# One reciprocal of two columns for the softmax sums of two neighbouring query tiles

## The chip, the cores and the metric

The kernel runs on one core of one Trainium2 chip. The metric is the time of one execution on the device in microseconds (us); lower is better. Engines are named as in the profile: PE (TensorE matmuls), PEld (its weight loads), DVE (VectorE), ACT (ScalarE), POOL (GpSimd) and SP (SyncE, which issues all DMAs here). A tile is 128 partitions wide; PSUM is used as eight tiles of 128x512 fp32 that the matmuls write into.

## The reference

One encoder layer is applied to two sequences of 512 tokens, with 1024 channels. The input is normalised, one wide product `h @ w_in` feeds four mixers (pooling, attention, convolution, Fourier) with their gates, the four branches are projected up, gated and summed, and an output product with a second normalisation follows. The change lies in the attention:

```
def attend(qblk):
    s = jnp.einsum('bqhd,bkhd->bhqk', qblk, k, preferred_element_type=jnp.float32) * scale
    p = jax.nn.softmax(s, axis=-1).astype(v.dtype)
    return jnp.einsum('bhqk,bkhd->bqhd', p, v)
```

There are 8 heads and, for each head of each sequence, 4 query tiles of 128 rows against 512 keys: 2 x 8 x 4 = 64 softmax tiles of 128x512.

## The kernel before, in words

Every fp32 product is made of three fp32r products of high and low halves (`mm3`), so nearly every operand is split first: `split(hi, lo, src)` copies the high half on ACT and subtracts it on DVE; where the source lies in SBUF and not in PSUM, the subtraction may go to DVE or POOL (`either`).

Work is written down as a program of units, in an order that weaves the long products (the bulk) with the side work. The layer runs in stages: input products of both sequences (to about 563 us of the profile), then the merge products of the four branches with the attention of sequence 0 and then of sequence 1 woven between them, then seven output products (`out_product`, in the order 1, 2, 7, 6, 5, 4, 3) and for each tile the last normalisation and residual (`final`).

For one softmax tile (head `h`, query tile `qt`) three units matter, with other work between them:

- `s_unit` multiplies queries and keys into a PSUM tile, takes the row maximum on DVE (TENSOR_REDUCE into `nmx`) and the exponential on ACT into `pr`, which also writes the row sum into `sm` (ACTIVATE and its ACTIVATION_READ_ACCUMULATOR).
- `n_unit` takes the reciprocal of the sum on DVE and multiplies `pr` by it. The multiplication may run on DVE (TENSOR_SCALAR) or ACT (ACTIVATE with scale): `rec.choice` leaves that to the planner.
- `t_unit` transposes `pr` on PE into PSUM and splits the result into `ph` and `pl` for the product with the values, `pv_unit`.

In `attention` the units of one step stand as s(h, qt), t(h-1, qt), n(h, qt): a tile is normalised just after its scores, and its transposes come four steps later.

The order on each engine isn't the program's. `_Recorder` records each operation as an atom with its dependences; `hoist` moves loads ahead, and `plan` then lists the atoms anew: it gives each a due time, keeps a clock for each engine with estimated durations, and takes next what is ready and most due. It picks the engine of every `choice`, and the buffers (caps: 42 halves of large tiles `b`, 16 tiles `g`, 10 small tiles `s`, 8 PSUM tiles). So one removed instruction can change what stands in a row on an engine, or which engine does it, hundreds of microseconds later. All recorded operations are issued by one line, L182, so the profile's groups are told apart by tiles: `ps` is PSUM, `b` large tiles, `g` tiles of 128x512, `s` small columns.

Of the kernel before, what the change touches and what calls it, by code (L numbers as in the profile page):

```python
# [14 lines left out]
AF = mybir.ActivationFunctionType  # L15
ALU = mybir.AluOpType
# [463 lines left out]
def trunk_kernel(ctx: ExitStack, tc: tile.TileContext, a: dict):  # L480
# [4 lines left out]
    rec = _Recorder()  # L485
# [9 lines left out]
    act, dve, pool, pe, sync = (Engine(e) for e in ("act", "dve", "pool", "pe", "dma"))  # L495
# [14 lines left out]
    def g_(dt=F32, w=512):  # L510
        return rec.new("g", (P, w), dt)
# [7 lines left out]
    def s_(w=1):  # L519
        return rec.new("s", (P, w), F32)  # L520

    def psum(tag):
        return rec.new("ps", (P, 512), F32)
# [45 lines left out]
    def mm3(out, lh, ll, rh, rl, first, last, **kw):  # L569
        pe.matmul(out, lh, rh, start=first, stop=False, **kw)  # L570
        pe.matmul(out, lh, rl, start=False, stop=False, **kw)
        pe.matmul(out, ll, rh, start=False, stop=last, **kw)
# [27 lines left out]
    def build(s):  # L600
        st = {}
# [16 lines left out]
        def Unit(fn, cost=0.0, chunks=()):  # L618
            return _Unit(fn, cost, [(0 if c[0] in SHARED or c[0] == "u" and c[1] < 6 else s,) + c for c in chunks])
# [3 lines left out]
        def after(*keys):  # L623
            assert all(k in done for k in keys), keys
# [248 lines left out]
        def s_unit(h, qt):  # L873
            def fn():
                after("kr0", "kr1", ("k", h // 2))
                qh, ql = [st["q", h // 2][:, h % 2, i] for i in range(2)]
                k = st["k"]
                t = slice(qt * P, (qt + 1) * P)
                p = psum("sc")
                mm3(p, qh[:, t], ql[:, t], k[:, h % 2, 0, :], k[:, h % 2, 1, :], True, True)  # L880
                nmx, sm, rc = s_(), s_(), s_()
                dve.tensor_reduce(nmx, p, axis=AX.X, op=ALU.max, negate=True)
                pr = g_()
                act.activation(pr, p, AF.Exp, bias=nmx, accum_out=sm)
                st["p", h, qt] = (pr, sm)
            return Unit(fn, 0.65)

        def n_unit(h, qt):
            def fn():
                pr, sm = st["p", h, qt]  # L890
                rc = s_()
                dve.reciprocal(rc, sm)
                rec.choice(dve=("tensor_scalar", (pr, pr, rc, None), dict(op0=ALU.mult)),
                           act=("activation", (pr, pr, AF.Copy), dict(scale=rc)))
            return Unit(fn, 0.0)

        def t_unit(h, qt):
# [939 lines left out]
```

## Time and profile before

| | us |
|---|---|
| median of 3 runs | 923.95 (922.61 to 928.17) |
| the profiled execution | 927.52 |
| its span, first to last instruction | 925.7 |
| PE busy | 898.8 (97%) |
| DVE busy | 721.9 (78%) |
| ACT busy | 492.2 (53%) |
| POOL busy | 359.4 (39%) |

The profiled execution is 1.8 us longer than its span, and 3.6 us longer than the median of the runs. Busy time counts overlapping instructions of an engine once; the duration of a single short DVE instruction overlaps with the next one, so the distance between two starts tells what it takes in a row of instructions.

### The profile page before, as it was taken

Reading aid. Unit: us, or ns where it says so; the run is one execution under the profiler, and the core shown is the slowest. Engines: PE = TensorE matmul, PEld = TensorE weight load, DVE = VectorE, ACT = ScalarE, POOL = GpSimd, SP = SyncE. Lnnn points to the kernel's source line nnn. Section 1 sums busy time; section 2 is a strip of 40 time slices with the busy share of each in tenths; the row PEclk is TensorE's granted clock in tenths of the full one; section 3 lists DMA queues with packets and bytes.
Section 4 is the critical chain, followed back from the end, with each engine's and each line's share of the span. In section 5 each row is a group of like instructions: output and inputs, shape, how many; then the busy total and the mean of one; then the engine's idle time right before and its main releaser. Section 6 shows DMA issues by size and latency. Waiting matters only on the chain. (4 is left out here: it accounts for less than half of the span.)

```text
span 925.7 us, 12147 instructions
## 1 busy us (share of the span) xinstructions
PE 898.8 (97%) x4125; PEld 725.4 (78%) x4125; DVE 721.9 (78%) x1089; ACT 492.2 (53%) x871; POOL 359.4 (39%) x305
## 2 busy tenths in 40 slices
PE   7999999999999999999999999899999999999996
PEld 6897877888778888877888887787778777777784
DVE  6889999689994655667634367978899778899998
ACT  7964233345443345435444456855676678873253
POOL 2798432126331322346100031412353344246935
PEclk9999999999999999999999999999999999999998
DMA  7140123332232333543322447866754564461124
GB/s 273 64 152 10 58 103 125 129 110 103 91 125 106 128 133 130 173 142 118 136 104 102 141 141 179 254 217 198 233 186 133 161 242 148 155 231 58 37 101 182
DMA packets 62258, 129.86 MB, mean 140 GB/s; under 512 B 6890, under 2 KB 10483, under 8 KB 61684
## 3 DMA queue, kind: packets, MB, share of 16 engines
q1 hardware_dynamic: 62196, 129.09, 41.7%
q8 instruction: 32, 0.52, 0.2%
q14 instruction: 30, 0.25, 0.1%
HBM read 88.56 MB, written 37.36 MB: 136 GB/s over the span
## 5 line engine op out<-in xcount | busy, mean ns | idle before, releaser
L182 PE MATMUL ps<-b,b 128*128 128x512 f32 (+3 forms) x3428 | 808.1, 392 | 9.9 <-DVE b L182 4.7
L182 PEld LDWEIGHTS ps<-b,b 128*128 128x128 f32 (+1 forms) x3428 | 626.5, 187 | 158.0 <-DVE b L182 6.7
L182 ACT ACTIVATE b<-b 128x1024 fp32r<-128x1024 f32 (+9 forms) x164 | 141.3, 880 | 127.6 <-PE ps L182 46.4
L182 POOL TENSOR_TENSOR b<-b,b 128x512 fp32r<-128x512 f32 (+4 forms) x79 | 120.8, 1542 | 141.1 <-ACT b L182 134.5
L182 DVE TENSOR_TENSOR b<-b,b 128x512 fp32r<-128x512 f32 (+5 forms) x167 | 144.5, 892 | 31.6 <-ACT b L182 30.6
L182 POOL TENSOR_TENSOR b<-g,b 128x512 fp32r<-128x512 f32 x48 | 69.0, 1442 | 133.3 <-ACT b L182 133.3
L182 DVE TENSOR_TENSOR g<-ps,g 128x512 f32<-128x512 f32 (+4 forms) x101 | 66.2, 658 | 63.6 <-PE ps L182 35.8
L182 ACT ACTIVATE g<-ps 128x512 f32<-128x512 f32 (+5 forms) x110 | 59.4, 542 | 88.3 <-PE ps L182 71.9
L182 DVE TENSOR_TENSOR b<-ps,b 128x512 fp32r<-128x512 f32 (+2 forms) x128 | 85.0, 682 | 21.2 <-ACT b L182 20.4
L182 DVE SCALAR_TENSOR_TENSOR ps<-b,cols,ps 128x512 f32<-128x512 f32 x116 | 87.3, 752 | 2.7
L182 ACT ACTIVATE b<-g 128x512 fp32r<-128x512 f32 x101 | 61.5, 629 | 32.3 <-DVE g L182 18.5
L182 ACT ACTIVATE b<-ps 128x512 fp32r<-128x512 f32 (+2 forms) x116 | 66.5, 593 | 19.9 <-PE ps L182 19.2
L182 DVE TENSOR_TENSOR b<-b 128x512 f32<-128x512 f32 (+4 forms) x69 | 61.9, 898 | 9.0 <-POOL g L182 4.0
L182 ACT ACTIVATE g<-ps,s 128x512 f32<-128x512 f32 (+1 forms) x77 | 48.5, 639 | 23.8 <-DVE s L182 14.9
L182 ACT ACTIVATE g<-g,cols 128x512 f32<-128x512 f32 x48 | 34.6, 721 | 48.7 <-DVE g L182 48.3
L182 POOL TENSOR_TENSOR b<-b 128x512 f32<-128x512 f32 (+3 forms) x32 | 43.7, 1367 | 39.2 <-DVE b L182 16.2
L182 POOL TENSOR_TENSOR b<-b,g 128x512 f32<-128x512 f32 x26 | 37.2, 1436 | 51.1 <-DVE g L182 36.0
L182 DVE TENSOR_TENSOR b<-g,b 128x512 fp32r<-128x512 f32 x53 | 51.2, 980 | 4.6 <-ACT b L182 4.1
L182 PE MATMUL ps<-b 128*128 128x512 f32 (+1 forms) x216 | 52.1, 388 | 1.2 <-DVE b L182 1.2
L182 POOL TENSOR_TENSOR g<-b 128x512 f32<-128x512 f32 x15 | 20.1, 1342 | 80.5 <-DMA b<-in_wt 47.7
L182 DVE TENSOR_REDUCE s<-ps 128x1 f32<-128x512 f32 x64 | 43.4, 681 | 4.9 <-PE ps L182 4.5
L182 PEld LDWEIGHTS ps<-b 128*128 128x128 f32 x216 | 39.5, 188 | 9.7 <-issue 1.4
(74 smaller groups left out, 563.4 us busy)
## 6 DMA issues: line engine op xcount, KB each, us to landing
st<-g SPq DMA_DIRECT2D x104, 256.0 KB, 2.0
b<-in_wt SPq DMA_DIRECT2D x50, 512.0 KB, 4.7
g<-st SPq DMA_DIRECT2D x100, 256.0 KB, 3.4
b<-in_x SPq DMA_DIRECT2D x15, 512.0 KB, 4.5
b<-in_wup SPq DMA_DIRECT2D x14, 512.0 KB, 4.5
b<-st SPq DMA_DIRECT2D x4, 1024.0 KB, 6.8
b<-in_wo SPq DMA_DIRECT2D x8, 512.0 KB, 6.7
out_y<-b SPq DMA_DIRECT2D x16, 256.0 KB, 2.1
```

The costliest lines, as they stand in the source:

```text
L182: getattr(engines[atom.eng], method)(*[real(x) for x in args], **{k: real(x) for k, x in kw.items()})
```

## The change

`s_unit` of an even query tile makes a small tile of two columns; the exponentials of the even and the odd tile write their sums into its two columns. `n_unit` of an even tile now does nothing; that of the odd tile takes one reciprocal of both columns and then multiplies both tiles, each by its own column.

```
-                nmx, sm, rc = s_(), s_(), s_()
+                nmx = s_()
+                if qt % 2 == 0:
+                    st["sm", h, qt // 2] = s_(2)
+                sm = st["sm", h, qt // 2][:, qt % 2:qt % 2 + 1]
...
         def n_unit(h, qt):
             def fn():
-                pr, sm = st["p", h, qt]
-                rc = s_()
-                dve.reciprocal(rc, sm)
-                rec.choice(dve=("tensor_scalar", (pr, pr, rc, None), dict(op0=ALU.mult)),
-                           act=("activation", (pr, pr, AF.Copy), dict(scale=rc)))
+                if qt % 2:
+                    rc = s_(2)
+                    dve.reciprocal(rc, st["sm", h, qt // 2])
+                    for i in range(2):
+                        pr, r = st["p", h, qt - 1 + i][0], rc[:, i:i + 1]
+                        rec.choice(dve=("tensor_scalar", (pr, pr, r, None), dict(op0=ALU.mult)),
+                                   act=("activation", (pr, pr, AF.Copy), dict(scale=r)))
```

The planner's new lists begin to differ at the first softmax tile and keep the same work: 64 reciprocals of one column become 32 of two; of the 64 multiplications 18 stand on DVE and 46 on ACT, where 8 and 56 stood; of the operations that may run on DVE or POOL, 33 went from DVE to POOL and 23 from POOL to DVE. On PE 726 of 740 groups of matmuls keep their place in the order; nine of the others stand one place earlier, and five stand one to four places later.

On DVE, at the first softmax tiles of sequence 0. `s_701` is the maximum of tile 0 of head 0, and the rows that follow are the maxima, reciprocals and multiplications of the next tiles; SCALAR_TENSOR_TENSOR is the low half of a query product. Before:

```order
L182 TENSOR_REDUCE s_701_4573<-ps_699_4565 128x1
L182 TENSOR_REDUCE s_703_4579<-ps_700_4569 128x1
L182 TENSOR_REDUCE s_709_4594<-ps_702_4575 128x1
L182 RECIPROCAL s_713_4604<-s_705_4582 128x1
L182 SCALAR_TENSOR_TENSOR b_706_4584<-ps_691_4507,b_706_4584 128x512
L182 TENSOR_REDUCE s_715_4615<-ps_708_4590 128x1
L182 RECIPROCAL s_718_4621<-s_712_4602 128x1
L182 TENSOR_REDUCE s_719_4623<-ps_710_4597 128x1
L182 RECIPROCAL s_720_4632<-s_717_4619 128x1
L182 TENSOR_SCALAR g_716_4618<-g_716_4618,s_720_4632 128x512
```

After:

```order
L182 TENSOR_REDUCE s_701_4573<-ps_699_4565 128x1
L182 TENSOR_REDUCE s_703_4579<-ps_700_4569 128x1
L182 TENSOR_REDUCE s_709_4594<-ps_702_4575 128x1
L182 SCALAR_TENSOR_TENSOR b_706_4584<-ps_691_4507,b_706_4584 128x512
L182 TENSOR_REDUCE s_714_4613<-ps_708_4590 128x1
L182 RECIPROCAL s_715_4616<-s_705_4582 128x2
L182 TENSOR_REDUCE s_716_4618<-ps_711_4599 128x1
L182 TENSOR_SCALAR g_712_4603<-g_712_4603,s_715_4616 128x512
```

The reciprocal of tile 0 is gone from its place; one of two columns stands where that of tile 1 stood, and the multiplication on DVE is now that of tile 1.

On DVE, in the output products, from the evacuation of product 6 on. The rows that read `ps` evacuate a PSUM tile twice (each into another sum); the others are low halves of operands of products 5, 4 and 3 (`b_1480_7703<-b_1414_7419` in the first list and `b_1448_7934` in the second are that of w_out's chunk 0 for product 4, the operand that product 4 needs first). Before:

```order
L182 TENSOR_TENSOR b_1510_8001<-b_1453_7550,b_1510_8001 128x512
L182 TENSOR_TENSOR b_1510_8001<-b_884_5313,b_1510_8001 128x512
L182 TENSOR_TENSOR b_1511_8010<-b_1446_7531,b_1511_8010 128x512
L182 TENSOR_TENSOR b_1511_8010<-b_884_5313,b_1511_8010 128x512
L182 TENSOR_TENSOR b_1499_7907<-ps_1501_7922,b_1499_7907 128x512
L182 TENSOR_TENSOR b_1407_7395<-ps_1501_7922,b_1407_7395 128x512
L182 TENSOR_TENSOR b_1512_8017<-b_1416_7433,b_1512_8017 128x512
L182 TENSOR_TENSOR b_1480_7703<-b_1414_7419,b_1480_7703 128x512
L182 TENSOR_TENSOR b_1499_7907<-ps_1502_7926,b_1499_7907 128x512
L182 TENSOR_TENSOR b_1407_7395<-ps_1502_7926,b_1407_7395 128x512
```

After:

```order
L182 TENSOR_TENSOR b_1436_7812<-ps_1438_7827,b_1436_7812 128x512
L182 TENSOR_TENSOR b_1351_7311<-ps_1438_7827,b_1351_7311 128x512
L182 TENSOR_TENSOR b_1436_7812<-ps_1439_7831,b_1436_7812 128x512
L182 TENSOR_TENSOR b_1351_7311<-ps_1439_7831,b_1351_7311 128x512
L182 TENSOR_TENSOR b_1428_7720<-b_1390_7454,b_1428_7720 128x512
L182 TENSOR_TENSOR b_1436_7812<-ps_1440_7835,b_1436_7812 128x512
L182 TENSOR_TENSOR b_1351_7311<-ps_1440_7835,b_1351_7311 128x512
L182 TENSOR_TENSOR b_1436_7812<-ps_1441_7839,b_1436_7812 128x512
L182 TENSOR_TENSOR b_1351_7311<-ps_1441_7839,b_1351_7311 128x512
L182 TENSOR_TENSOR b_1442_7894<-b_871_5292,b_1442_7894 128x512
L182 TENSOR_TENSOR b_1447_7929<-b_1357_7344,b_1447_7929 128x512
L182 TENSOR_TENSOR b_1448_7934<-b_1354_7328,b_1448_7934 128x512
```

The low half that product 4 needs first stood behind two evacuations of product 6; it now stands behind all eight.

On POOL, over the same stretch: the low halves for products 5, 4 and 3, from the first that reads chunk 3 of the summed operands on. Before:

```order
L182 TENSOR_TENSOR b_1480_7703<-b_808_4987,b_1480_7703 128x512
L182 TENSOR_TENSOR b_1512_8017<-b_884_5313,b_1512_8017 128x512
L182 TENSOR_TENSOR b_1513_8046<-b_1453_7550,b_1513_8046 128x512
L182 TENSOR_TENSOR b_1513_8046<-b_875_5282,b_1513_8046 128x512
L182 TENSOR_TENSOR b_1518_8114<-b_1518_8114,g_1366_7223 128x512 x2
```

After:

```order
L182 TENSOR_TENSOR b_1417_7608<-b_797_4963,b_1417_7608 128x512
L182 TENSOR_TENSOR b_863_5263<-b_863_5263,b_790_4940 128x512
L182 TENSOR_TENSOR b_1417_7608<-b_797_4963,b_1417_7608 128x512
L182 TENSOR_TENSOR b_1442_7894<-b_1390_7454,b_1442_7894 128x512
L182 TENSOR_TENSOR b_1428_7720<-b_1385_7438,b_1428_7720 128x512
L182 TENSOR_TENSOR b_1408_7558<-b_871_5292,b_1408_7558 128x512
L182 TENSOR_TENSOR b_1447_7929<-b_871_5292,b_1447_7929 128x512
L182 TENSOR_TENSOR b_1448_7934<-b_863_5263,b_1448_7934 128x512
L182 TENSOR_TENSOR b_1449_7952<-b_863_5263,b_1449_7952 128x512
L182 TENSOR_TENSOR b_1451_7986<-b_1357_7344,b_1451_7986 128x512
L182 TENSOR_TENSOR b_1451_7986<-b_863_5263,b_1451_7986 128x512
L182 TENSOR_TENSOR b_1417_7608<-b_863_5263,b_1417_7608 128x512
```

Three operations stood between the low half of product 5's chunk 2 (the first row of each list) and the first multiplication by the output gain (the last row before); twelve stand there now (one more follows the rows shown), ten of them moved from DVE.

## Rows read from the trace of the kernel before

**Rows 1.** The page of the profile: busy time of the engines, and busy tenths of PE and DVE in 40 equal slices of the span (23 us each).

```profile
PE 898.8 (97%) x4125; PEld 725.4 (78%) x4125; DVE 721.9 (78%) x1089; ACT 492.2 (53%) x871; POOL 359.4 (39%) x305
...
PE   7999999999999999999999999899999999999996
...
DVE  6889999689994655667634367978899778899998
```

**Rows 2.** Busy time of each engine in stretches of the span, which begin where the softmax begins: first and last us and the length, then PE, PEld, DVE, ACT and POOL, the granted clock of PE, the share of the DMA engines and GB/s.

```profile
563.00:600.00 37.00, 34.09 (x169) 26.93 (x168) 32.22 (x56) 30.75 (x63) 13.32 (x12) 1.00 0.81 227
600.00:720.00 120.00, 118.29 (x621) 95.03 (x620) 104.53 (x184) 77.34 (x150) 38.31 (x32) 1.00 0.59 191
720.00:760.00 40.00, 37.71 (x175) 28.22 (x173) 30.52 (x57) 28.93 (x57) 18.35 (x14) 1.00 0.67 219
760.00:840.00 80.00, 78.59 (x390) 62.23 (x389) 70.95 (x116) 61.87 (x125) 35.04 (x26) 1.00 0.48 162
840.00:900.00 60.00, 59.91 (x259) 48.14 (x258) 58.29 (x72) 24.91 (x52) 40.06 (x27) 1.00 0.21 71
```

**Rows 3.** What PE waited for from 563 us to the end: total us, times, longest.

```profile
PE ps L182 <- DVE b L182: 5.5, 9, 1.7
PE ps L182 <- ACT g L182: 1.2, 2, 0.6
...
PE ps L182 <- DVE g L182: 0.4, 1, 0.4
PE ps L182 <- DVE s L182: 0.4, 1, 0.4
```

**Rows 4.** The timeline of PE: start, us of the merged piece, instructions; in brackets the idle time before it and what ended it. Waits behind the softmax's start.

```profile
587.54 3.74 PE L182 MATMUL ps<-b,b 128*128 128x512 f32 x14 [0.25 <-DVE b L182]
...
596.87 2.33 PE L182 MATMUL ps<-b,b 128*128 128x512 f32 x9 [1.75 <-DVE b L182]
...
739.81 0.95 PE L182 MATMUL ps<-b,b 128*128 128x512 f32 x3 [0.59 <-ACT g L182]
...
752.38 2.35 PE L182 MATMUL ps<-b,b 128*128 128x512 f32 x9 [0.81 <-DVE b L182]
...
822.04 5.74 PE L182 MATMUL ps<-b 128*128 128x512 f32 x24 [1.16 <-DVE b L182]
```

**Rows 5.** Groups of instructions by shape from 563 us to the end, on DVE (two rows) and ACT (one): busy us and mean ns of one, then the idle time before them and what ended it.

```profile
L182 DVE RECIPROCAL s<-s 128x1 f32<-128x1 f32 x64 | 9.6, 153 | 1.6 <-ACT g L182 1.4
L182 DVE TENSOR_SCALAR g<-g,s 128x512 f32<-128x512 f32 x8 | 5.5, 689 | 0.3
...
L182 ACT ACTIVATE g<-g,s 128x512 f32<-128x512 f32 x56 | 40.4, 722 | 12.5 <-DVE s L182 12.4
```

**Rows 6.** The timeline of DVE at the first softmax tiles of sequence 0, and some 26 us later where the low half of a transposed tile (`b<-ps,b`) stands behind a small copy.

```profile
568.05 0.15 DVE L182 RECIPROCAL s<-s 128x1 f32<-128x1 f32 x1
568.12 0.69 DVE L182 TENSOR_REDUCE s<-ps 128x1 f32<-128x512 f32 x1
568.78 0.16 DVE L182 RECIPROCAL s<-s 128x1 f32<-128x1 f32 x1
568.98 0.49 DVE L182 TENSOR_SCALAR g<-g,s 128x512 f32<-128x512 f32 x1
...
594.34 1.80 DVE L182 COPY g<-g 128x2 f32<-128x2 f32 x1
596.05 0.68 DVE L182 TENSOR_TENSOR b<-ps,b 128x512 fp32r<-128x512 f32 x1
```

**Rows 7.** The first transposes of a softmax tile on PE, of sequence 0 and of sequence 1, and between them the reciprocal on DVE of tile 1 of sequence 1.

```profile
571.48 0.60 PE L182 MATMUL ps<-ident,g 128*128 128x128 f32 x4
...
726.53 0.15 DVE L182 RECIPROCAL s<-s 128x1 f32<-128x1 f32 x1
...
729.66 0.60 PE L182 MATMUL ps<-ident,g 128*128 128x128 f32 x4
```

**Rows 8.** DVE groups by shape in two stretches of the output products: from 868 to 881 us, in which POOL works without a break, and from 881.5 to 886 us, in which it rests.

```profile
L182 DVE TENSOR_TENSOR b<-b,b 128x512 f32<-128x512 f32 x3 | 5.3, 1780 | 0.0
L182 DVE TENSOR_TENSOR b<-ps,b 128x512 f32<-128x512 f32 x4 | 2.5, 676 | 0.0
...
L182 DVE TENSOR_TENSOR b<-b,b 128x512 fp32r<-128x512 f32 x7 | 4.3, 686 | 0.1
```

**Rows 9.** The timelines of POOL and PE there.

```profile
865.86 14.83 POOL L182 TENSOR_TENSOR b<-b,b 128x512 f32<-128x512 f32 x9
886.21 1.30 POOL L182 TENSOR_TENSOR b<-b,b 128x512 fp32r<-128x512 f32 x1 [5.52 <-ACT b L182]
...
883.83 2.91 PE L182 MATMUL ps<-b,b 128*128 128x512 f32 x12
...
894.73 0.85 PE L182 MATMUL ps<-b,b 128*128 128x512 f32 x3
```

**Rows 10.** The end of the timelines of PE and DVE.

```profile
916.07 0.84 PE L182 MATMUL ps<-b 128*128 128x512 f32 x3
...
916.98 0.68 DVE L182 TENSOR_TENSOR b<-b,b 128x512 f32<-128x512 f32 x1
917.59 0.68 DVE L182 TENSOR_TENSOR b<-ps,b 128x512 f32<-128x512 f32 x1
...
919.78 2.73 DVE L182 SCALAR_TENSOR_TENSOR b<-b,s,b 128x512 f32<-128x512 f32 x4
```

## Prediction, written before the changed kernel ran

> **What bounds the kernel now.** The page comes first: PE is busy for 97% of the span, in every slice but the first and last few, and DVE for 78% [rows 1]. The change touches nothing ahead of the first softmax tile at 563 us, where the two lists of instructions are still the same, so only the rest counts. There the table by stretches gives PE's idle time as length less busy time: 37.0 - 34.1 = 2.9 us, then 1.7, 2.3, 1.4 and 0.1 us, together 8.4 us of 337 [rows 2]. PE is the bound from 563 to 900 us, and what is not PE's own work is those 8.4 us and the tail behind its last matmul. What ends PE's waits is nearly always DVE: 5.5 + 0.4 + 0.4 us of them, and 1.2 us are ACT's exponentials [rows 3]. Most of the waiting matmuls need a PSUM tile that DVE has not yet emptied [rows 4]. DVE is also nearly full at the end: 58.3 of 60 us from 840 to 900 us [rows 2].
>
> That bounds the gain before any detail: if every one of those waits went, 8.4 us or 0.9% would be won. A loss has no such bound.
>
> The prediction is made against the profiled execution, 927.5 us with a span of 925.7 us; the median of the runs lies 3.6 us lower, and the same difference is put on it.
>
> **The change part by part.**
>
> *Reciprocals.* 32 of 64 go. Each is listed with 153 ns [rows 5], but behind one the next instruction starts 0.07 us later (568.05 to 568.12 us, rows 6), so DVE is freed of 32 x 0.07 = 2.2 us, not of 4.9. The remaining ones have two columns; no row has one of that shape. From below it costs what one column does, from above it costs twice the 0.07 us, which would take the 2.2 us back. I take the lower end, because DVE rows of 512 columns take 0.68 us, about 1 ns a column. Spread over 260 us of attention, 2.2 us of DVE reach PE only where they stand in the row that leads to one of DVE's eleven waits: a few times 0.07, under 0.5 us.
>
> The Trainium skill ("Perfetto Trace Analysis", section Optimizing Scalar/DVE Operations) says that grouping small operations into larger ones helps if the engine is saturated, and that where it is not but causes bubbles elsewhere, breaking instructions up may finish work sooner. By the first half the gain would be the 2.2 us of DVE; by the second the pair is a loss, which is the third rival.
>
> *The added wait.* The even tile's multiplication now waits for the odd tile's exponential. Behind it, on ACT or DVE, stand exponentials, evacuations and splits in order. Who needs the even tile first is its transpose on PE. In sequence 0 the reciprocal of tile 1 ran at 568.05 us [rows 6] and the transposes of tile 0 began at 571.48 us; in sequence 1 these are 726.53 and 729.66 us [rows 7]. That is 3.4 and 3.1 us of cover. I followed all 32 pairs so: these two are the smallest, every other has 4.9 us or more. One reciprocal and two multiplications of 0.72 us [rows 5] take 1.6 us, so the wait is hidden, at no cost. If the two smallest covers failed, each would cost its part over 3 us.
>
> *Fewer waits on ACT.* ACT stood idle 12.4 us in front of its 56 multiplications, waiting for reciprocals [rows 5]. Now the second of a pair finds its column ready, so up to half, 6 us of ACT, is given back, and exponentials may come earlier. PE's waits for exponentials are 1.2 us in all [rows 3]; I credit none here, 1.2 us at most.
>
> *Multiplications to DVE.* Ten more stand on DVE. One took 0.49 us where it ran undisturbed [rows 6] and 0.69 in the mean [rows 5]: 5 to 7 us more on DVE. The operations that went to POOL, ten more than came back, free DVE of 10 x 0.6 = 6 us. With the 2.2 us of the reciprocals DVE's load in total falls by 1 to 3 us, and order decides, not load.
>
> The Trainium skill ("SBUF — State Buffer", section Who interferes with whom) says that of DVE operations with one SBUF input just copies and tensor_scalar can take the port pair that GpSimd needs, and that the later of the two then waits for the whole of the other. By that the ten multiplications would each meet POOL; the mean of 0.69 against 0.49 us fits for some of the eight, and if all ten waited for a POOL operation of 1.3 us the sum would be 10 us higher on DVE, not on PE.
>
> *560 to 600 us.* PE's wait of 1.75 us at 596.87 ended when DVE had emptied a transposed tile at 596.05 to 596.73, which had stood behind a copy of two columns that took 1.80 us [rows 4, 6]. In the new list this split stands ahead of that copy: up to 1.2 us won. Ahead of the first value product (587.54 us) stand now two low halves of the Fourier table on DVE, which POOL did before: 2 x 0.6 us, up to 1 us lost in its wait of 0.25. Net -0.3 us, from -1.3 to +1.0.
>
> *600 to 720 us.* A multiplication now stands on DVE in front of the split that the value product of head 2 waits for: +0.4 us; nothing else that PE waited for has moved. Taken +0.2, from -0.5 to +1.0.
>
> *720 to 760 us.* In front of the first split of sequence 1 stand two low halves that POOL did; DVE had idle time there (30.5 of 40 us busy, rows 2). The exponential that PE waited 0.59 us for at 739.81 [rows 4] now stands behind one more evacuation on ACT, +0.5 us; against that, the large split ahead of the wait of 0.81 us at 752.38 starts sooner. Net 0, from -1.0 to +1.2.
>
> *760 to 840 us.* The wait of 1.16 us at 822.04 [rows 4] is for a split on DVE which had one multiplication and two reciprocals in front of it that are gone, while one evacuation of 0.6 us has come: -0.5 us, from -1.2 to +0.8.
>
> *840 to 900 us.* Ten low halves go from DVE to POOL. What that costs is in rows 8: a DVE operation with both inputs in SBUF took 1.78 us while POOL worked without a break [rows 8, 9], and 0.69 us while it rested; one that reads PSUM took 0.68 us even then. The two engines take turns in such operations. POOL needs 14.83 / 9 = 1.65 us each in such turns, and 1.30 alone [rows 9]. Now POOL has work from 880 to beyond 897 us, so the DVE operations of that stretch fall into turns. The operand that product 4 needs first, at 894.73 us [rows 9], is now split behind all eight evacuations of product 6. Its last four PSUM tiles are done between 883.83 and 883.83 + 2.91 = 886.7 us, the first at about 884.7. DVE empties each twice, at 0.6 us: eight times make 4.8 us, one low half between them 0.6 to 1.7, so 890.1 to 891.2; then three low halves at 0.6 to 1.7: 891.9 to 896.3. PE wants it at 894.73: from 0 to 1.6 us of a new wait. I take +0.8. POOL's own last operand for product 4 is the seventh from 882.9 us, at 1.3 to 1.74 each 892 to 895 us: no more than that.
>
> *Tail.* PE's last matmul ends at 916.9 us, and its evacuation started only at 917.59 us, behind another operation [rows 10]. It now stands directly behind the small column that it had followed at a distance, and may start 0.5 us sooner; but two residual operations that had been done by then come behind it, 0.60 + 0.66 us, ahead of the last four of 2.73 us. Net +0.4 us, from -0.5 to +1.0.
>
> **Sum:** -0.3 + 0.2 + 0 - 0.5 + 0.8 + 0.4 = +0.6 us; ends -4.5 and +6.6 us if all fell together. The profiled execution would take 928.1 us, the median 924.5 us. What separates this kernel from no change in a measurement is about 1%, 9.2 us, so this is no change.
>
> **The rivals.**
>
> 1. *Slower: POOL and DVE in turns.* 33 operations moved to POOL, and each DVE operation that meets one costs 1.78 - 0.68 = 1.1 us more [rows 8]. It decides only where such an operation leads to a matmul or to the last store. If from 870 us on it delays DVE by 9 such turns on PE's path, the time is 924 + 10 = 934 us. For it: DVE is 97% busy there [rows 2], with little slack. Against it: ten operations left DVE there, and only three of the remaining ones lie on the path to product 4. Chance 0.05.
>
> 2. *Faster: DVE's waits go.* DVE ended 6.3 of the 8.4 us [rows 3]; if the new order and the lighter row remove two thirds, 4 us, of them and nothing comes instead, the time is 920 us, still within 1%. For it: the longest wait has its cause, the 1.80 us copy, moved behind. Against it: what was in front of other splits is only exchanged for other work. Chance 0.15. More than 9.2 us is out of reach of the 8.4 us, unless the tail shortens too: 0.02.
>
> 3. *Pairs come late.* The even tile's result is held back for the odd one's, and its transposes wait. The cover is 3.1 us at the least [rows 6, 7]; if both first heads lost 2 us each and the busy ACT queues of the following heads two more, the time is 924 + 6 = 930 us. Chance 0.08, since a pair needs 1.6 us. It is what the second half of the rule on grouping in the Trainium skill ("Perfetto Trace Analysis") amounts to.
>
> **How the numbers follow.** The forecast itself has 0.70: 924.5 us, from about 921 to 928. With rival 2 below and rival 3 above, the range that leaves out no more than 2 in 10 is 919.5 to 929.5 us: below, nearly the whole -4.5 us of the sum; above, most of the +6.6 us, less the unlikely case that all ends meet. Rival 1 (0.05) lies outside. Faster by over 1%: 0.02. Slower by over 1%: 0.05, rival 1. Within 1%: 0.93, the forecast, rival 3 and nearly all of rival 2.
>
> **What would show it.** In the profile after: RECIPROCAL x32 with a mean near 153 ns; no wait of PE's transposes (`ps<-ident,g`) on ACT or DVE `g`; PE's idle time from 563 to 900 us again near 8.4 us, with the 1.75 us wait at 597 us shorter; a new wait of PE near 895 us ended by DVE or POOL `b`; DVE's `b<-b,b` of 128x512 near 1.7 us between 882 and 898 us; the last DVE operation 0 to 1 us later. The prediction is wrong if PE's idle time there is above 15 us or below 3 us, if transposes wait, or if two columns cost DVE far more than one.

## The result, and the profile after

The changed kernel took 931.64 us (median of 6 runs, 929.44 to 933.62), the kernel before beside it 926.78 us (6 runs, 922.61 to 928.17): 1.0057 times as long, with a 95% interval from 1.0038 to 1.0076. That is a loss of 0.57%, inside the "within 1%" that had been given 0.93, but outside the range of 919.5 to 929.5 us, and it can be told from no change. Five executions of the whole series, the profiled one of the eighth experiment among them, took 1.6 to 5.4 times as long as the others of their kernels; all medians and ratios leave them out, and nothing is read from that profile. The profiled execution took 931.99 us with a span of 930.2 us, 4.5 us longer than the span before.

The page shows no engine that became the bound: PE and DVE work as long as before, ACT 6.8 us less and POOL 15.9 us more [rows 1].

```profile
PE 898.3 (97%) x4125; PEld 724.7 (78%) x4125; DVE 721.7 (78%) x1057; ACT 485.4 (52%) x861; POOL 375.3 (40%) x315
```

The groups by shape are those of [rows 5]; a reciprocal of two columns costs what one of one column did (157 against 153 ns), and ACT waits 7.5 us in front of its multiplications where it waited 12.4.

```profile
L182 ACT ACTIVATE g<-g,s 128x512 f32<-128x512 f32 x46 | 31.4, 717 | 7.5 <-DVE s L182 7.5
L182 DVE TENSOR_SCALAR g<-g,s 128x512 f32<-128x512 f32 x18 | 11.3, 630 | 0.8
L182 DVE RECIPROCAL s<-s 128x2 f32<-128x2 f32 x32 | 4.9, 157 | 1.4 <-ACT g L182 1.4
```

So the reciprocals and ACT's waits for them came out as forecast, and the time went elsewhere. The table by stretches (columns as in [rows 2]) tells where: PE's idle time is 2.9, 4.2, 3.3, 1.3 and 0.2 us, together 11.9 us where it was 8.4.

```profile
563.00:600.00 37.00, 34.06 (x171) 27.07 (x170) 31.97 (x52) 29.52 (x60) 16.40 (x14) 1.00 0.78 225
600.00:720.00 120.00, 115.81 (x602) 91.55 (x602) 101.20 (x166) 74.67 (x147) 38.70 (x33) 1.00 0.59 187
720.00:760.00 40.00, 36.72 (x174) 28.64 (x174) 32.95 (x57) 25.35 (x52) 13.34 (x10) 1.00 0.72 225
760.00:840.00 80.00, 78.69 (x394) 62.61 (x393) 70.58 (x112) 60.69 (x122) 32.26 (x24) 1.00 0.48 165
840.00:900.00 60.00, 59.83 (x258) 47.64 (x257) 58.38 (x63) 24.21 (x48) 52.06 (x34) 1.00 0.20 71
```

The waits of PE from 563 us on (as [rows 3]) name DVE 11 times as before, but for 9.9 us in all where it was 6.3, and one of 2.5 us is longer than any of before:

```profile
PE ps L182 <- DVE b L182: 6.9, 9, 1.4
PE ps L182 <- DVE g L182: 3.0, 2, 2.5
PE ps L182 <- ACT g L182: 1.3, 3, 0.6
```

On PE's timeline these are the waits that count, in the notation of [rows 4]:

```profile
594.06 0.93 PE L182 MATMUL ps<-b,b 128*128 128x512 f32 x3 [1.12 <-DVE b L182]
...
599.37 6.64 PE L182 MATMUL ps<-b,b 128*128 128x256 f32 x45 [1.41 <-DVE b L182]
...
608.17 3.44 PE L182 MATMUL ps<-b,b 128*128 128x512 f32 x18 [0.81 <-DVE b L182]
612.04 0.66 PE L182 MATMUL ps<-ident,g 128*128 128x128 f32 x4 [0.42 <-DVE b L182]
...
719.12 0.66 PE L182 MATMUL ps<-ident,g 128*128 128x128 f32 x4 [0.56 <-DVE b L182]
...
755.45 0.96 PE L182 MATMUL ps<-b,b 128*128 128x512 f32 x3 [2.53 <-DVE g L182]
...
825.54 2.77 PE L182 MATMUL ps<-b 128*128 128x512 f32 x11 [1.28 <-DVE b L182]
```

How far the same matmul lies behind its place in the kernel before is a better measure than idle time, because groups of matmuls that follow without a wait overlap by some 0.14 us in the listing, so that a listed wait costs PE that much more than its number. The first transposes of the softmax lie 0.18 us earlier than before, the first Fourier product at 599.4 us 0.03 us earlier, the last value product of sequence 0 (718.59 before, 722.62 after) 4.03 us later; the matmul of 752.38 [rows 4] lies 4.27 us later, that of 822.04 now stands at 825.54 (3.50 later), that of 894.73 [rows 9] at 898.48 (3.75), and DVE's last four instructions start at 924.15 and not at 919.78 us [rows 10] (4.37). Nearly all of the loss is made between 600 and 720 us, and a second one, at 755 us, takes the place of waits that the kernel before had nearby.

**At 608 us.** DVE stood idle 2.65 us in front of the evacuation of a merge tile:

```profile
604.38 0.40 DVE L182 TENSOR_TENSOR g<-ps,g 1x256 fp32r<-1x256 f32 x1
607.43 0.69 DVE L182 SCALAR_TENSOR_TENSOR b<-g,ps 128x512 f32<-128x512 f32 x1 [2.65 <-PE ps L182]
```

The line names PE, but the matmul that made this tile had ended at 604.6 us; the other operand, a gate tile `g`, comes from memory and landed at 607.34 us. SyncE's timeline shows why it came late. In the changed kernel (first three lines) the 1 MB of queries of heads 4 and 5 (`b<-st`) is issued at 599.01 us and the gate tiles behind it from 601.25; in the kernel before (last two lines) the gate tiles are the second and third load of the row at 599.71, and the queries stand behind them:

```profile
598.64 0.32 SPq L182 DMA_DIRECT2D g<-st  x1
599.01 0.42 SPq L182 DMA_DIRECT2D b<-st  x1
601.25 2.41 SPq L182 DMA_DIRECT2D g<-st  x3
```

```profile
599.71 1.27 SPq L182 DMA_DIRECT2D g<-st  x3
601.03 0.42 SPq L182 DMA_DIRECT2D b<-st  x1
```

There the same evacuation ran at 605.45 us with no idle time before it. Now PE waits at 608.17 us for the tile that this evacuation empties, and at 612.04 for that of a later one, which DVE started at 611.30 us.

**At 755 us.** ACT stood 2.76 us in front of the split of a key chunk, waiting for its load. Behind it stand, in order, two multiplications, the split of another chunk, that of a value tile, an exponential, and the copy of the first value product of sequence 1 at 753.86:

```profile
750.10 0.42 ACT L182 ACTIVATE g<-b 128x256 fp32r<-128x256 f32 x1 [2.76 <-DMA b<-in_wk]
750.42 1.32 ACT L182 ACTIVATE g<-g,s 128x512 f32<-128x512 f32 x2
751.65 1.04 ACT L182 ACTIVATE b<-b 128x1024 fp32r<-128x1024 f32 x1
752.60 0.57 ACT L182 ACTIVATE b<-ps 128x512 fp32r<-128x512 f32 x1
753.08 0.67 ACT L182 ACTIVATE g<-ps,s 128x512 f32<-128x512 f32 x1
753.64 0.20 ACT L182 ACTIVATION_READ_ACCUMULATOR g<-ps,s 128x1 f32 x1
753.86 0.59 ACT L182 ACTIVATE g<-ps 64x512 f32<-64x512 f32 x1
```

DVE's sum behind that copy empties the tile that PE waits for. The chain of waits of the changed kernel says the same in three of its pieces:

```profile
745.09 4.99 DMA b<-in_wk
...
750.10 1.66 ACT g L182 x3
...
755.45 4.68 PE ps L182 x23
```

In the kernel before, this load was issued at 740.37 us and the split ran at 745.56 without a wait; now it is issued at 745.09, behind two more gate tiles.

**Between 661 and 684 us** the profile shows some 2 us more, in small waits behind a merge chunk whose load landed late: ACT stood 1.60 us for it at 664.61 us, the load having been issued at 658.29. In the second experiment's profile, whose lists differ only in the split reciprocals, it was issued at 657.10 and ACT did not wait, so the lists alone do not force this wait.

### The profile page after: what moved, and what is told of

Same layout as the page of the kernel before. It is cut to its first block, busy times and chain, and to the rows that moved or that the text cites. A ratio compares the mean times of both kernels' runs of the same rounds, so it can differ in the third digit from the quotient of the medians.

```text
span 930.2 us, 12128 instructions
## 1 busy us (share of the span) xinstructions
PE 898.3 (97%) x4125; PEld 724.7 (78%) x4125; DVE 721.7 (78%) x1057; ACT 485.4 (52%) x861; POOL 375.3 (40%) x315
## 5 line engine op out<-in xcount | busy, mean ns | idle before, releaser
L182 POOL TENSOR_TENSOR b<-b,b 128x512 fp32r<-128x512 f32 (+3 forms) x89 | 138.6, 1573 | 135.3 <-ACT b L182 132.0
L182 DVE TENSOR_TENSOR b<-b,b 128x512 fp32r<-128x512 f32 (+7 forms) x157 | 143.4, 938 | 29.8 <-ACT b L182 29.0
L182 POOL TENSOR_TENSOR b<-g,b 128x512 fp32r<-128x512 f32 x45 | 64.4, 1435 | 118.1 <-ACT b L182 118.1
L182 ACT ACTIVATE g<-ps 128x512 f32<-128x512 f32 (+4 forms) x111 | 59.7, 540 | 87.6 <-PE ps L182 70.7
L182 DVE TENSOR_TENSOR b<-b 128x512 f32<-128x512 f32 (+4 forms) x69 | 59.7, 867 | 9.9 <-POOL g L182 5.0
L182 DVE TENSOR_TENSOR b<-g,b 128x512 fp32r<-128x512 f32 x56 | 55.5, 1005 | 3.9 <-ACT b L182 3.2
L182 PE MATMUL ps<-b 128*128 128x512 f32 (+1 forms) x192 | 47.3, 388 | 1.3 <-DVE b L182 1.3
L182 PE MATMUL ps<-ident,g 128*128 128x128 f32 (+1 forms) x281 | 43.0, 273 | 4.0 <-DMA g<-in_pre 2.6
```

What stands on the lines that cost most here:

```text
L182: getattr(engines[atom.eng], method)(*[real(x) for x in args], **{k: real(x) for k, x in kw.items()})
```

## Experiments

Each was timed in 5 rounds beside the kernel before (medians 926.4 to 927.5 us); ratios are to it, with a 95% interval. "Lists" are the orders that the planner makes for the engines and for SyncE. Edits of the lists stand behind the planner's call.

**1 and 2: the lists and the pairs, crossed.** The first keeps the lists of before and puts the pairs on them:

```
+    for i, (even, odd) in enumerate(pairs.values()):
...
+        odd[1].calls = [("reciprocal", (rc, sm), {})]
+        order.remove(even[1].n)
+        order.remove(even[2].n)
+        order.insert(order.index(odd[1].n) + 1, even[2].n)
```

> The lists of every engine are those of the kernel before; only then are the sums of two neighbouring tiles put side by side: 32 reciprocals of one column go, 32 of two columns stand where the odd tile's stood, and the even tile's multiplication stands right behind it, on the engine that it had. Theory A (the loss comes from the lists that the planner makes anew, not from the pairing): 924.5 to 927.5 us, PE's idle time between 600 and 720 us within 1 us of the 2.4 us of before (120 us less 118.29 busy is 1.7 us by the windows). Rival B (the pairing itself: even tiles are normalised later, two multiplications stand behind each other on ACT): 929 to 933 us, with PE or the splits of the probabilities waiting for the even tiles.

Measured: 932.95 us, 1.0065 (1.0045 to 1.0085). Theory A missed: pairs on the old lists cost as much as the change did. The profile shows one place for half of it. ACT, at 668 us, comes to the even tile's multiplication and stands 3.13 us, because the reciprocal of the pair (tiles 0 and 1 of head 5) runs only at 671.05. What stands behind it on ACT's list comes later too, among it an exponential of 675.27 us. The transposes at 676.11 us wait until that exponential, which reads a PSUM tile, is done, and the matmuls behind them run slowly:

```profile
671.23 0.73 ACT L182 ACTIVATE g<-g,recips 128x512 f32<-128x512 f32 x1 [3.13 <-DVE recips L182]
...
675.27 0.69 ACT L182 ACTIVATE g<-ps,s 128x512 f32<-128x512 f32 x1
```

```profile
671.18 2.34 PE L182 MATMUL ps<-b,b 128*128 128x512 f32 x9
...
676.11 0.93 PE L182 MATMUL ps<-ident,g 128*128 128x128 f32 x4 [1.79 <-ACT g L182]
676.69 3.51 PE L182 MATMUL ps<-b,b 128*128 128x512 f32 x8
```

The transposes that wait are not those of the late tile: they belong to tile 3 of head 4, whose reciprocal ran at 656.12 us. Those of the late tile came at 683.51 us and waited for nothing. So what is lost here is lost through the queue of ACT.

Nine matmuls had taken 2.34 us; eight now take 3.51. In the windows (length, PE busy, granted clock, DMA share, GB/s) the granted clock is at half, 1.2 GHz, behind that wait, and back after some 3.4 us:

```profile
676.00:677.00 1.00, 0.90 (x5) 0.67 0.14 53
677.00:678.00 1.00, 1.00 (x4) 0.50 0.06 16
678.00:679.00 1.00, 1.00 (x4) 0.50 0.88 205
679.00:680.00 1.00, 1.00 (x4) 0.62 0.52 131
680.00:681.00 1.00, 1.00 (x6) 1.00 1.00 283
```

The second keeps the lists of the changed kernel and splits each reciprocal:

```
+            rc, sm = x.calls[0][1]
+            x.calls = [("reciprocal", (rc[:, j:j + 1], sm[:, j:j + 1]), {}) for j in range(2)]
```

> The lists are those of the changed kernel, but each reciprocal of two columns is written as two of one column, one right behind the other. Theory A: the lists carry the loss and DVE has room, so 931 to 933 us, within 0.2% of the changed kernel. Rival B gives the same. A third reading (the saved instructions are a gain that the lists eat up): 32 instructions at 0.07 to 0.16 us on DVE, at most 2.2 to 5 us if all of it lay on the path: 934 to 937 us.

Measured: 931.24 us, 1.0058 (1.0037 to 1.0078). The 32 saved instructions are worth nothing that can be measured here. In this profile PE's wait at 754 us (2.62) was followed by a fall of the clock, which the changed kernel's was not.

**3 and 4: other lists.** The third changes one number, `win=115` to `win=114`. The fourth gives every operation of the changed kernel the engine that it has in the kernel before.

> The kernel before, with its work untouched; only the planner's window is 114 atoms in place of 115, so that it makes its lists anew with about as many differences as the change brought (62 choices of an engine, 16 places on PE). Theory A: such a list alone moves the time by some microseconds, to either side: at least 2 us away from the kernel before, somewhere in 922 to 934 us. Rival B: nothing is paired, so within 1.5 us of the kernel before, 925 to 928 us.

Measured: 931.55 us, 1.0059 (1.0040 to 1.0078): a new order alone, with no pair in it, costs as much as the change. Most of it is one wait, at a place where neither kernel had any, and the slow matmuls behind it (twelve in 4.60 us). It lies before the softmax, so it is none of the places where the change loses its time:

```profile
78.69 4.60 PE L182 MATMUL ps<-b,b 128*128 128x512 f32 x12 [2.49 <-ACT g L182]
```

> The changed kernel, but every operation that has a choice of engine is given the one that it has in the kernel before (64 multiplications and 746 others); the planner still orders them. If the choices of engine carry the loss (the copy of the first value product on ACT at 753 us, ten more operations on POOL): 925 to 928 us. If the order in which the lists stand carries it (theory A without the choices): 929 to 934 us. Rival B: 930 to 933 us.

Measured: 937.98 us, 1.0117 (1.0095 to 1.0139), worse than both readings foresaw. Choices of engine made for one order and forced on another cost more here, with waits of 2.89 and 2.32 us that neither kernel has. So this run does not tell whether the choices or the order carry the change's own loss.

**5 and 6: two places, undone and done.** In the changed kernel:

```
+    move((0, "far", 2), (1, "g", 2, 2), 1)
+    move((1, "pv", 0), (1, "copied", 0), 1)
+    for x in ((1, 1, 0), ((0, "u", 9),), ((1, "kn", 1),)):
+        for part in ("lo", "hi"):
+            move((part, *x), (1, "pv", 0), 1)
```

`move(x, y, 1)` puts x directly behind y: the queries' load behind the gate tiles, and the two chunks' splits and a value tile's behind the value product's copy and sum.

> The changed kernel with two places of its lists put right, nothing else. First, the load of the queries of heads 4 and 5 (1 MB) stands behind the two gate tiles of the third merge column again, as in the kernel before, and not ahead of them. Second, on ACT the splits of the key chunk and of the last merge chunk and of a value tile, which stood ahead of an exponential and of the copy of the first value product of sequence 1 and waited 2.8 us for a load, stand behind them. Theory A (the loss is in waits that the new lists make, at places that can be named): PE's waits at 608 and 612 us (0.81 and 0.42) go, that at 755 us (2.53) falls below 1 us; 927.5 to 929.5 us. Rival B (the pairing itself): within 1 us of the changed kernel, 930.5 to 933 us.

Measured: 928.17 us, 1.0030 (1.0010 to 1.0051), in the range of theory A. The waits at 608 and 612 us are gone, and so is that at 755, but not without a successor: the tile that PE needs next is split late on ACT, at 750.07 us, behind 0.72 us of waiting for the low half of one of the moved chunks (DVE, 748.76 us). The wait that was to fall below 1 us thus came back with 2.18:

```profile
605.66 3.82 PE L182 MATMUL ps<-b,b 128*128 128x258 f32 x24
609.31 0.60 PE L182 MATMUL ps<-ident,g 128*128 128x128 f32 x4
...
751.53 0.63 PE L182 MATMUL ps<-ident,g 128*128 128x128 f32 x4 [2.18 <-DVE b L182]
```

Two places thus carry 0.27 of the 0.57%, by the two ratios; the difference is known only to lie between about 0 and 0.55%. The sixth puts the two loads of the kernel before where the changed kernel has them:

```
+    move((0, "far", 2), (0, "g", 2, 2))
+    move((1, "kn", 1), (0, "g", 1, 2), 1)
```

> The kernel before, nothing paired, with only two loads moved on SyncE's list to where the changed kernel has them against their neighbours: the 1 MB of queries of heads 4 and 5 ahead of the gate tiles of the third merge column, and the key chunk of sequence 1 behind the gate tiles of columns 1 and 2 of the last branch. Theory A: DVE's evacuation at 605 us waits for its gate tile (about 2 us, PE 0.5 to 1.2 us), ACT waits 2 to 4 us at 746 us for the key chunk (PE 1 to 2.5 us at about 755 us): 928 to 931 us. Rival B: two loads among 417 cost nothing, 925 to 928 us.

Measured: 930.21 us, 1.0038 (1.0019 to 1.0057), as theory A had it: two loads of 417, with nothing paired, cost 3.5 us. PE waits 0.78 us at 608.69 and 1.72 at 746.87, and ACT waits for the key chunk:

```profile
ACT g L182 <- DMA b<-in_wk: 2.5, 1, 2.5
```

**7 and 12: where the even tile stands.** The seventh is the first with the even tile's multiplication ahead of the odd tile's; the twelfth has that place too, but nothing shared, each reciprocal in its old place.

```
-        order.insert(order.index(odd[1].n) + 1, even[2].n)
+        order.insert(order.index(odd[2].n), even[2].n)
```

> As the first experiment (pairs on the lists of the kernel before), but the even tile's multiplication stands directly ahead of the odd tile's and not directly behind the reciprocal, so that on ACT nothing waits for the reciprocal earlier than it did. If the 6 us of the first experiment came from the place on ACT (a multiplication that stood 3.13 us at 668 us with splits queued behind it): 925 to 928 us. If they come from the pairing (even tiles normalised late, whatever the place): 930 to 934 us, with the transposes still waiting for the even tile at 672 us.

Measured: 930.28 us, 1.0035 (1.0017 to 1.0054): at the lower edge of the second reading. The place on ACT was part of the first experiment's loss, not all (0.30% less, with an uncertainty nearly as large). The transposes at 672 us that the expectation took for those of an even tile are again those of tile 3 of head 4.

> The lists of the kernel before, nothing paired: each tile has its own reciprocal in its old place, but the even tile's multiplication stands directly ahead of the odd tile's, as in the seventh experiment. If what the pairs cost there (930.28 us, 3.9 above the kernel before) is that the even tile is normalised late: 929 to 931.5 us. If it is the shared sums and the one reciprocal: 925.5 to 927.5 us.

Measured: 929.10 us, 1.0011 (0.9991 to 1.0031). This cannot be told from the kernel before, nor clearly from the seventh, so the pair was measured again below.

**8 and 11: more lists.** The eighth and the eleventh change three numbers of the planner, and one.

> The changed kernel with three numbers of the planner a little different (ahead 19.285 for 19.873, aheado 19.635 for 19.833, bias 0.562 for 0.517), so that it makes other lists for the same paired work. Theory A (the loss belongs to one set of lists): some microseconds away from the changed kernel to either side, 925 to 935 us, and not bound to 931. Rival B: never below 929 us, since every list carries the pairs.

Measured: 932.88 us, 1.0067 (1.0041 to 1.0092). Another list for the paired work is no better.

> The kernel before, nothing paired, with one number of the planner different (aheado 20.813 for 19.833), so that it makes other lists. Theory A (most lists that the planner makes are some microseconds worse than those of the kernel before, paired or not): 928 to 934 us. Rival B (unpaired work is faster): 925 to 928 us. Below 925 us would say that the lists of the kernel before were nothing special.

Measured: 926.99 us, 1.0000 (0.9981 to 1.0019). Here theory A missed, but the test was weaker than meant: these lists are those of the kernel before up to about 750 us, where 20 operations change their engine, none of them on PE. It says that another order of that last part costs nothing, and nothing of the stretch in which the changed kernel loses most. The third experiment's lists differ from the start, and cost 0.6%.

**9 and 10: single instructions of DVE's list.** The ninth is the kernel before with one low half ahead of the 1.80 us copy of [rows 6]:

```
+    move(("t", 0, 1, 0), ("fold", 0, 1))
```

> The kernel before, nothing paired, with one instruction of DVE's list a place earlier: the low half of tile 0 of head 1 stands ahead of the copy of two columns at 594.34 us that took 1.80 us (it ends with the POOL instruction beside it), and not behind it. Theory A (single places of the lists carry microseconds): PE's wait at 596.87 us (1.75) falls below 0.5 us, and with it goes the fall of the granted clock that followed this wait in three of the experiments: 924 to 926 us, 0.5 to 2.5 us under the kernel before. If PE only meets its next wait: 926 to 927 us.

Measured: 925.43 us, 0.9982 (0.9966 to 0.9999), faster than both kernels. On DVE the copy now stands behind the low half and still takes 1.72 us:

```profile
594.75 0.69 DVE L182 TENSOR_TENSOR b<-ps,b 128x512 fp32r<-128x512 f32 x1
595.35 1.72 DVE L182 COPY g<-g 128x2 f32<-128x2 f32 x1
```

The wait at 596.87 us is gone, but in this profile PE met one of 1.36 us at 598.51, and at 599 us it is not ahead (0.27 us behind); its gain appears only further on. Its runs lie between 923.9 and 926.9 us, those of the kernel before beside it between 923.1 and 931.6. A fall of the granted clock to half for 3.4 us, as in the first experiment, lowers the mean clock of an execution of 926 us by 0.0018. The mean over these runs is 0.9972, over the kernel before beside them 0.9953, so one such fall less in each execution would fit the gain. In the profiles of the first, sixth, seventh and twelfth experiments, where the copy stands ahead of the low half, PE waits 1.89 to 2.19 us at about 596 us and such a fall follows each time; in that of the kernel before none follows. That the moved low half spares this fall is thus likely, but not shown.

The tenth is the fifth with two low halves on DVE put earlier:

```
+    move(("lo", 0, 1, 0), ("copied", 0, 0))
+    move(("t", 0, 1, 1), ("t", 0, 1, 0), 1)
```

> The fifth experiment (changed kernel, two places put right) with two more: on DVE the low half of a value tile that kept PE waiting at 593.2 us (1.11) stands ahead of a copy of columns, and the low half of tile 1 of head 1, behind which PE waited at 598.65 us (1.56), stands four places earlier. Theory A: those 2.7 us fall to below 1 us, so 925.5 to 927.5 us, no slower than the kernel before although every pair is there. Rival B (the pairs cost something that no place of the lists explains): 928 us, as the fifth experiment.

Measured: 928.71 us, 1.0011 (0.9995 to 1.0027). By the ratio it cannot be told from the kernel before, though all 32 pairs are in it; nor can it be told from the fifth. The waits of 1.11 and 1.56 us did not fall below 1 us as expected: 1.20 and 0.85 us and a smaller one stand in their place, for other tiles.

**13 and 14: the price of a pair.** On the lists of the ninth, the pairs of the seventh (13) and the late even tiles of the twelfth (14).

> The lists of the ninth experiment (kernel before with one low half a place earlier on DVE, 925.4 us), with the pairs of the seventh: shared sums, one reciprocal of two columns, the even tile's multiplication directly ahead of the odd tile's. If pairs cost what the waits for even tiles add in the profile of the seventh experiment (six waits of PE for ACT's tiles, 2.2 us in all, where the kernel before had two of 1.2 us, and four new waits for DVE of some 0.5 us that stand in for old ones): 926.5 to 928 us. If pairs cost 3.9 us of themselves: 928.5 to 930 us. If they cost nothing: 925 to 926.5 us.

Measured: 928.83 us, 1.0021 (1.0005 to 1.0036). Against the ninth (0.9982) that is 0.39% or 3.6 us for the pairs (from the two intervals about 0.16 to 0.62%), more than their waits had promised. The waits of PE for ACT's tiles grow from 3 of 2.3 us in the ninth to 8:

```profile
PE ps L182 <- ACT g L182: 3.3, 8, 0.8
```

One is at 672 us, the place of the first experiment, and again the transposes that wait are those of tile 3 of head 4, not those of a late tile:

```profile
672.20 0.66 PE L182 MATMUL ps<-ident,g 128*128 128x128 f32 x4 [0.47 <-ACT g L182]
```

> The same lists and the same place of the even tile's multiplication, but each tile with its own reciprocal in its old place. If lateness is the whole price of a pair: within 1 us of the run beside it (the thirteenth). If half of the price is the shared reciprocal (both tiles wait for the later exponential's sum): 1 to 2 us under it.

Measured: 928.15 us, 1.0020 (1.0007 to 1.0033), the same as with pairs. The wait at 672 us is not in this profile. The price is the late even tile; sharing sums and reciprocal adds nothing that can be measured. Nearly half of it has a place. In all five runs with late even tiles on the old lists (1, 7, 12, 13 and 14) three waits, which neither the kernel before nor the ninth has, put PE 1.5 to 1.8 us further behind; in the fourteenth they are:

```profile
770.23 0.66 PE L182 MATMUL ps<-ident,g 128*128 128x128 f32 x4 [0.45 <-DVE b L182]
...
786.30 0.66 PE L182 MATMUL ps<-ident,g 128*128 128x128 f32 x4 [0.40 <-ACT g L182]
...
799.40 0.95 PE L182 MATMUL ps<-b,b 128*128 128x512 f32 x3 [0.24 <-ACT g L182]
```

Here too no transpose waits for its own tile's multiplication. The first wait ends with an evacuation on DVE that stood behind a late multiplication of 1.36 us (768.22 us), the second with an exponential on ACT that stood behind two multiplications in a row (783.78 and 784.40 us).

## Why the prediction was wrong

*The base, too low.* The median of 924.5 us was built on 923.95 us, the median of three runs; six runs of the same kernel now gave 926.78. Of the 7.1 us between 924.5 and 931.64, 2.8 are this base, and the change itself was worth +4.9 us where +0.6 was forecast. On the new base the range would have been 922.3 to 932.3 us and would have held the result, but only because it was wide: the step named below failed all the same.

*Reciprocals, right.* Two columns cost what one does, and 32 fewer of them are worth nothing (second experiment). Here the forecast's "under 0.5 us" held. The dearer multiplications on DVE did not come: ten waits of 1.3 us would make 13 us and not 10, and the 18 multiplications took 0.63 us in the mean.

*The added wait, right for the changed kernel, wrong as a statement on pairs.* Its transposes of even tiles wait for no multiplication; the planner placed the work around them. But "hidden, at no cost" had been read from covers of 3.1 us and more, counting one reciprocal and two multiplications. The first experiment shows what was left out: an engine that takes its list in order. ACT stood 3.13 us in front of a multiplication, with exponentials and splits behind it. On fixed lists the late tiles cost 3.6 us (experiments 13 and 14). That is rival 3 in part, which had been given 0.08: its direction is right where the planner doesn't move other work, its 6 us are too many, and its way is another. No transposes of a late tile waited for its own multiplication, not even in the two first heads, with covers of 3.45 and 3.73 us in the first experiment; other work, queued behind the late multiplications on ACT and DVE, came late. The second half of the rule of the Trainium skill ("Perfetto Trace Analysis", section Optimizing Scalar/DVE Operations) says that breaking instructions up may finish work sooner where an engine causes bubbles elsewhere. Breaking up alone won nothing here: a reciprocal for each tile gave 1.0058 against 1.0057 (second experiment) and 1.0020 against 1.0021 (fourteenth). What these runs show is the order: tiles normalised at once are ahead of tiles held back by 0.38 to 0.39%.

*560 to 600 us, near.* Forecast -0.3 us, measured +0.15, counted from the first transposes of the softmax on. The wait of 1.75 us did go, and 1.12 and 1.41 us came instead.

*600 to 720 us: this step failed.* It read "nothing else that PE waited for has moved", +0.2 us and at most +1.0; it measured +4.1 us in this profile. The step had followed only what PE waited for before. The new waits were for things that had been in time: a gate tile behind 1 MB of queries (608 us). On the order of DMAs the working had nothing at all, though 70 of 417 stand elsewhere in the new list. Some 2 of the 4.1 us need not come with these lists: the second experiment's profile loses 1.6 us in this stretch, still more than the +1.0 allowed. The time of that kernel was the same none the less; in its profile the wait at 754 us and the fall of the clock behind it cost 3.3 us, where that at 755 us cost 1.6 in the changed kernel's.

*720 to 760 us, right in sum, not in kind.* Forecast 0, measured +0.2 us: a wait of 2.53 us, made by the key chunk's late load, replaced all others. That it costs more than this profile tells is seen in the second experiment, where the clock fell behind it.

*760 to 840 us*: forecast -0.5, measured -0.8. *840 to 900 us*: forecast +0.8 for a new wait at 895 us, measured +0.25 and no such wait. POOL works there without a break from 862.79 us for 34.16 us, and DVE's low halves take 1.41 us in the mean where they took 0.69, as foreseen from [rows 8]; DVE was in time for product 4 all the same, since its eight evacuations began at 886.32 us with PE 3.7 us behind, some 2 us sooner against PE than the 884.7 us reckoned with; the low half that product 4 needs ended at 895.78 us, and the product came at 898.48. *Tail*: forecast +0.4, measured +0.6 us.

The sum of +0.6 us was thus a sum of known places with one missing kind of place. None of the signs that were named would have told: PE's idle time of 11.9 us lies between the 3 and 15 us allowed, and the transposes that waited (612.04 and 719.12) waited for evacuations, not for multiplications. Rival 1 can be dropped, since in this profile the turns of POOL and DVE reached no matmul; rival 2 saw the removal of the longest wait rightly. The ninth experiment, which removes only that, was 0.18% faster (0.01 to 0.34), though its profile doesn't show the gain at that place.

What is settled: the changed lists lose at places that can be named (experiments 5 and 6), and a loss of this kind needs no pairs (3 and 6). What stays open is how much of the 4.9 us is due to the pairs in the changed lists. With four places mended the changed kernel is between 0.05% faster and 0.27% slower than the kernel before (experiment 10), in which nothing is mended; against the ninth, with one place mended, it is 0.29% slower (about 0.06 to 0.52). On the old lists the pairs cost 0.35 and 0.39% (7, and 13 against 9). The two are not parts of one sum, because the planner makes other lists for late tiles.

## What to carry to other kernels

Where a planner orders the work, a change is to be costed by what stands in front of each instruction in its new list, loads included, and not by the waits of the old profile: those show only what was late before. An engine that takes its list in order passes a wait on to all that stands behind it, so an operation that must wait for a later partner belongs behind what need not wait. And before a small gain or loss is put down to a change, the same planner should be run with one number altered: here one such number gave +0.6%, and another, which changed the lists only from about 750 us on, nothing.

## What had not been expected of the hardware

Behind long waits of PE the granted clock fell to 1.2 GHz and then rose again, in the first experiment after 3.4 us. In the profiles of the two kernels and of the experiments but the eighth, PE waited 18 times between 1.72 and 2.89 us behind the start-up and before the tail, and in 14 of them the clock fell behind it. In the first experiment the transposes at 676.11 us stood 3.78 us behind their place in the kernel before (672.33), and matmuls at 679.80 us 5.22 us behind theirs (674.58): 1.4 us on top of the wait. The same wait was followed by a fall in one execution and not in another (2.62 us at 754 us in the second experiment, 2.53 at 755 us in the changed kernel), which is part of the spread of the runs: of 97 executions of the kernel before, the 26 with a mean granted clock of 0.997 or more took 925.0 us in the mean, the 44 with 0.995 or less 927.9.

A copy of two columns on DVE took 1.80 us in the kernel before and 1.72 in the ninth experiment, where others took 0.16; it ended within 0.03 us of the POOL operation beside it each time (596.14 and 596.11, 597.07 and 597.04 us). In the eleventh experiment the copy began 0.12 us before that POOL operation and took 0.19.
